# Where tiles lie in SBUF: weight slots and moving activation tiles put on fixed offsets modulo 256 bytes

## The chip, the cores and the metric

The kernel runs on one core of one Trainium2 chip. The metric is the device time of one execution in microseconds (us); several executions are timed and the median is given. Beside the times there is one execution taken by the hardware profiler, from which the tables below come. In them PE is the matrix engine (its matmuls), PEld its weight loads, DVE the vector engine, ACT the scalar engine, POOL the GpSimd engine and SP the engine that issues the DMAs. SBUF is the on-chip memory of 128 partitions; an address below is a byte within a partition, the same in all 128.

## The reference

The program is a two-layer encoder trunk on 256 tokens of width 1024, in float32. Each layer adds three sub-layers to the stream `h`: a gated feed-forward network (FFN) of width 2816, a token-mixing sub-layer with three head groups, and a second FFN. Before each stands an RMSNorm with a shift and scale computed from a vector `c`.

```python
for l in range(DEPTH):
    mod = (cond @ ada_w[l] + ada_b[l]).reshape(B, 9, D_MODEL)[:, None]
    u = modulate(rmsnorm(h, norm_ffn1[l]), mod[:, :, 0], mod[:, :, 1])
    h = h + 0.5 * (1.0 + mod[:, :, 2]) * swiglu(u, ffn1_wg[l], ffn1_wu[l], ffn1_wd[l])
    u = modulate(rmsnorm(h, norm_mix[l]), mod[:, :, 3], mod[:, :, 4])
    proj = u @ w_in[l]
    ...
    mixed = jnp.concatenate([y_ret, y_sb, y_ssm], axis=-1) @ w_out[l]
    h = h + (1.0 + mod[:, :, 5]) * mixed
    u = modulate(rmsnorm(h, norm_ffn2[l]), mod[:, :, 6], mod[:, :, 7])
    h = h + 0.5 * (1.0 + mod[:, :, 8]) * swiglu(u, ffn2_wg[l], ffn2_wu[l], ffn2_wd[l])
```

`swiglu(u, wg, wu, wd)` is `(silu(u @ wg) * (u @ wu)) @ wd`. Retention, stick-breaking attention and the state-space mixer, which lie between `proj` and `mixed`, are small beside the matrix products with the weights.

## The kernel before

**The matrix products.** Every product with a weight matrix is made from three matmuls in the format fp32r: weights and activations are each split into a high part (`hi`, `uh`, the first half of `g`) and a remainder (`lo`, `ul`, the second half of `g`), and `mm3` (L200) issues hi·high, hi·low and lo·high into one PSUM bank. The weight block of 128x128 is the stationary operand (512 bytes of a partition), the activation chunk of 128x256 is the moving one (1024 bytes). Each matmul has a weight load of its own, so that in an instruction stream of matmuls a weight load for the next one runs beside each of them.

**The stages.** An FFN goes through 11 units of 256 columns: `proj` (L548) computes gate `pg` and up `pu` for one unit from `uh` and `ul` (48 matmuls each), the gated result is split into a `g` tile (`gated`, L570), and `out_unit` (L498) multiplies a `g` tile of an earlier unit into `dn` (48 matmuls: 24 for the unit's first half, then 24 for its second). The first four chunks of work after each norm are done by `lead` (L452) on tiles `hgh` and `hgl`, that hold h before the norm factor is known, with two columns more (258). The mixing sub-layer projects 20 units (`pj`, or `pv` with the operands swapped: there the weights are the moving operand and `uh`, `ul` the stationary one) and ends with six units of `wo`, whose moving tiles are the pairs `rh`/`rl`, `bh`/`bl` and `sh`/`sl`.

**The weights.** A DMA on SP's queue brings one unit of 1 MB into a raw tile (four to ten of 8192 bytes per partition). `step` (L255) takes half a unit at a time: ACT writes `hi` (L306), DVE writes `lo` (L307). Pools `whi` and `wlo` have eight slots each, and half number k goes into slot k mod 8 of both. The stream of vectors for `mod` (`raw_a`, L266 on DVE) shares the raw tiles and the queue. The order of all instructions on all engines is written out by the program (`manual_schedule`).

**Where tiles lie.** A pool's slots follow each other in SBUF, and pools and constant tiles follow each other in the order in which they are declared; sizes are rounded up to 32 bytes. The first 16384 bytes are a scratch area for DMAs. A weight slot has 1056 float32, so 4224 bytes, which is 128 more than a multiple of 256: the eight slots of `whi` and of `wlo` lie in turn at 160 and 32 modulo 256 bytes. Chunks within a slot are 1024 bytes apart, weight blocks 512, so that they keep the slot's offset. `uh` and `ul` lie at 128. Pool `k4` has ten slots that are sized by the largest tile, 4x258 float32 or 4128 bytes; slot 0 begins at 160, and each further one 32 later: 160, 192, 224, 0, 32, 64, 96, 128, 160, 192. The tiles `g`, `rh` to `sl`, `hgh`, `hgl` and the activations of the mixing sub-layer take these slots in turn. In `hgh` and `hgl` chunks are 1032 bytes apart.

Of the kernel before, what the change touches and what calls it, by code (L numbers as in the profile page):

```python
# [7 lines left out]
F32 = mybir.dt.float32  # L8
FR = mybir.dt.float32r
# [4 lines left out]
P = 128  # L14
# [42 lines left out]

ONES, IDENT, LATER, HIDDEN = range(4)
GS = 3
MIX_UNITS = ['z0', 'z1', 'sk0', 'sv0', 'x0', 'sq0', 'x1', 'x2', 'sq1', 'sk1', 'rv0', 'sv1', 'x3', 'rq0', 'rg0', 'rv1', 'rg1', 'rk0', 'rk1', 'rq1']  # L60
PAUSE = {'step_sizes': (4, 2), 'conv': (3,), 'values': (6, 0), 'state_scores': (4, 2), 'ssm': (2, 2, 1, 2, 2, 2, 0, 4, 4, 2, 2), 'stick': (2, 2, 5, 3, 0, 3, 3, 1), 'rope': (2,), 'retain': (2, 2, 2, 0, 4, 3, 5, 2)}
W_OUT_ORDER = (2, 3, 5, 4, 0, 1)
# [3 lines left out]
def ffn_order(first=False):  # L66
    g0 = GS if first else 1
    seq = []
    for j in range(NJ):
        seq += [("g", j), ("u", j)]  # L70
        if j >= g0:
            seq += [("d", i) for i in downs(j, g0)]
    return seq + [("d", NJ - 1)]
# [10 lines left out]
def weight_order():  # L84
    seq = []
    for l in range(L):
        seq += [(l, "ffn1") + it for it in ffn_order(l == 0)]
        seq += [(l, "mix", "in", n) for n in MIX_UNITS]
        seq += [(l, "mix", "out", n) for n in W_OUT_ORDER]
# [12 lines left out]

HSEQ = [(_w, _f) for _f in range(2) for _w in range(2 * GS)]
PAIRS = LEADS[1:] + [_w + 2 for _w in LEADS[1:]]
for _w in range(2 * GS, NW):
    if _w in PAIRS:
# [10 lines left out]
def stream_order():  # L117
    after = {}

    def spread(first, last, count):  # L120
        for i in range(count):
            w = first + (i * (last - first)) // max(1, count)
            after[w] = after.get(w, 0) + 1

    base = 0
    for l in range(L):
        for off, span in zip((0, NF, NF + NM), ADA_SPANS[l]):
            spread(base + off + span[1], base + off + span[2], span[0])
        base += NSUB
    seq = []  # L130
    for it in START.split():
        if it[0] in "xsn":
            seq.append((it, 0, 0))
        elif it[0] == "a":
            seq.append(("a", int(it[1:]), 0))
        else:
            seq += [("w",) + h for h in HSEQ[2 * int(it):2 * int(it) + 2]]
    a = 8
    for n, hf in HSEQ[4 * GS:]:
        seq.append(("w", n, hf))  # L140
        if hf:
            for _ in range(after.get(n, 0)):
                seq.append(("a", a, 0))
                a += 1
    assert a == NA
    return seq


SEQ = stream_order()
START_SEQ = SEQ[:11 + 4 * GS]  # L150
UNIT_OF = {it: i // 2 for i, it in enumerate(HSEQ)}
# [4 lines left out]
class Trunk:  # L156
# [5 lines left out]
    def __init__(self, ctx, tc, io):  # L162
        self.tc, self.nc, self.io = tc, tc.nc, io
        pool = lambda name, bufs, **kw: ctx.enter_context(tc.tile_pool(name=name, bufs=bufs, **kw))
        self.cp = pool("const", 1)
        self.rawp = pool("raw", self.NRAW)
        self.hip = pool("whi", self.NHALF)
        self.lop = pool("wlo", self.NHALF)
        self.t2 = pool("t2", 5)
        self.sm = pool("small", 2)  # L170
        self.ring = pool("ringp", 4, space=PSUM)
        self.pool = pool
        self.early = tc.tile_pool(name="early", bufs=self.NEARLY)
        self.earlyp = self.early.__enter__()
        self.raw = {}
        self.w = {}
        self.sent = 0
        self.done = 0
        self.ready = -1
        self.procs = []  # L180
        self.table = None
# [36 lines left out]
    def acc2(self, name):  # L218
        return self.accp.tile([P, 2, 512], F32, tag="acc", name=name)

    def tk4(self, name, dt=F32, w=256):
        return self.k4.tile([P, 4, w], dt, tag="k4", name=name)

    def tk3(self, name, dt=F32):
        return self.t3.tile([P, 2, 384], dt, tag="t3", name=name)
# [29 lines left out]
    def step(self):  # L255
        nc = self.nc
        kind, n, hf = SEQ[self.done]
        self.done += 1
        unit = UNIT_OF[n, hf] if kind == "w" else n
        while (kind, unit) not in self.raw:  # L260
            self.send()
        raw = self.raw[kind, unit]
        if kind == "a":
            for f in range(2):
                j = 2 * n + f
                nc.vector.tensor_tensor_reduce(  # L266
                    out=raw[:, f * 1024:(f + 1) * 1024], in0=raw[:, f * 1024:(f + 1) * 1024], in1=self.cond,
                    scale=1.0, scalar=self.par("ada_b", j), op0=ALU.mult, op1=ALU.add,
                    accum_out=self.mods[:, j:j + 1])
            del self.raw[kind, n]  # L270
            self.send()
            return
        hi = self.hip.tile([P, 1056], FR, tag="hi", name=f"hi{n}_{hf}")
        lo = self.lop.tile([P, 1056], FR, tag="lo", name=f"lo{n}_{hf}")
        l, _, what, which = WSEQ[n]
        part = HPOS[n, hf] % 2
        src = raw[:, part * 1024:(part + 1) * 1024]
        if (what, which) == ("in", "sv0"):
            hv, lv = (t.rearrange("p (k c) -> p k c", c=264) for t in (hi, lo))
            self.split(hv[:, :, 0:256], lv[:, :, 0:256], src.rearrange("p (k c) -> p k c", c=256))  # L280
            self.split(hv[:, :, 256:264], lv[:, :, 256:264], self.wdt[:, l, 4 * hf:4 * hf + 4])
            self.w[n, hf] = (hv, lv)
        else:
            hv, lv = hi[:, 0:1024], lo[:, 0:1024]
            self.split(hv, lv, src)
            if what not in ("d", "out"):
                hv, lv = (t.rearrange("p (k c) -> p k c", c=256) for t in (hv, lv))
            self.w[n, hf] = (hv, lv)
        self.ready = HPOS[n, hf]
        if part:  # L290
            del self.raw[kind, unit]
            self.send()
# [16 lines left out]
    def setup(self):  # L309
        nc, io = self.nc, self.io  # L310
        self.params = self.cp.tile([P, NPAR], F32, name="params")
        self.consts = self.cp.tile([P, NCST], F32, name="consts")
        self.cond = self.cp.tile([P, 1024], F32, name="cond")
        self.wdt = self.cp.tile([P, L, 8, 8], F32, name="wdt")
        self.mods = self.cp.tile([P, NA * 2], F32, name="mods")
        self.h = self.cp.tile([P, KD, S], F32, name="h")
        self.uh = self.cp.tile([P, KD, S], FR, name="uh")
        self.ul = self.cp.tile([P, KD, S], FR, name="ul")
        self.rs = self.cp.tile([P, S], F32, name="rs")
        self.mats = self.cp.tile([P, 4, P], FR, name="mats")  # L320
        self.eps = self.cp.tile([P, 1], F32, name="eps")
        nc.vector.memset(self.eps, EPS)
        nc.sync.dma_start(out=self.cond, in_=io["c"].broadcast_to([P, 1024]))
        nc.sync.dma_start(out=self.params, in_=io["params"])
        for _ in range(self.NRAW + self.NEARLY + 1):
            self.send()
        self.silu(out=self.cond, in_=self.cond)
# [16 lines left out]
    def norm_prep(self, gain, gi, shift, scale, lead=True):  # L344
        nc = self.nc
        self.gs = self.sm.tile([P, 8], F32, tag="gs", name="gs")
        nc.vector.scalar_tensor_tensor(out=self.gs, in0=self.mods[:, scale:scale + 8], scalar=1.0,
                                       in1=self.par(gain, gi, 8), op0=ALU.add, op1=ALU.mult)
        self.shift = shift
        self.sq = []  # L350
        self.hg = None
        if lead:
            self.hg = [(self.tk4("hgh", FR, 258), self.tk4("hgl", FR, 258)) for _ in range(2)]
            for i, (hi, lo) in enumerate(self.hg):
                src = self.mods[:, shift + 4 * i:shift + 4 * i + 4].unsqueeze(2).to_broadcast([P, 4, 2])
                self.split(hi[:, :, 256:258], lo[:, :, 256:258], src)

    def start(self, gain, gi, shift, scale):
# [5 lines left out]
        nps = self.acc("nps")  # L364
        banks = [self.bank("ld") if i < 4 else self.acc("ld") for i in range(2 * GS)]
        units, steps, new = 2 * GS, [0] * 8, [0] * 4
# [260 lines left out]
    def mix(self, l, w0, gate_col, prep):  # L627
# [299 lines left out]
        n = w0 + 2  # L927
        for idx, name in enumerate(MIX_UNITS):
            if idx < 2:
                continue  # L930
            done = []
            if idx == 2:
                ts = [target(name), target(MIX_UNITS[3])]
                self.proj2(n, *ts)
                done = [evac(name, ts[0]), evac(MIX_UNITS[3], ts[1])]
            elif idx > 3:
# [158 lines left out]
```

## Time and profile before

| | |
|---|---|
| time, median of 3 runs | 1163.01 us (1162.42 to 1163.47) |
| profiled execution, first to last instruction (span) | 1161.9 us, 22045 instructions |
| mean granted TensorE clock | 0.998 |
| PE matmuls busy | 1126.8 us, 97% of the span, 9316 matmuls |
| DVE busy | 893.3 us, 77% |
| ACT busy | 619.0 us, 53% |
| HBM read | 280.15 MB, 242 GB/s over the span |

Matmuls are pipelined: one's duration in the profile (280 ns) overlaps with the next one's, so the rate of the stream is read from the distance between the starts of matmuls and not from durations. The timeline prints the start of each row, and a row "x2" is two matmuls of the same tiles in a row. For the unit of an FFN it is enough to look at the first matmul of 24 and the one that follows the 24th.

### The profile page before, as it was taken

Reading aid. Unit: us, or ns where it says so; the run is one execution under the profiler, and the core shown is the slowest. Engines: PE = TensorE matmul, PEld = TensorE weight load, DVE = VectorE, ACT = ScalarE, POOL = GpSimd, SP = SyncE. Lnnn points to the kernel's source line nnn. Section 1 sums busy time; section 2 is a strip of 40 time slices with the busy share of each in tenths; the row PEclk is TensorE's granted clock in tenths of the full one; section 3 lists DMA queues with packets and bytes.
Section 4 is the critical chain, followed back from the end, with each engine's and each line's share of the span. In section 5 each row is a group of like instructions: output and inputs, shape, how many; then the busy total and the mean of one; then the engine's idle time right before and its main releaser. Section 6 shows DMA issues by size and latency. Waiting matters only on the chain.

```text
span 1161.9 us, 22045 instructions
## 1 busy us (share of the span) xinstructions
PE 1126.8 (97%) x9316; PEld 1115.7 (96%) x9316; DVE 893.3 (77%) x1300; ACT 619.0 (53%) x870; POOL 0.2 (0%) x4
## 2 busy tenths in 40 slices
PE   1999999999999999999999999999999999999996
PEld 1999999999999999999999999999999999999996
DVE  6988786788778788898488788667886877977544
ACT  4464434586874464444466444457687546544432
POOL 0000000000000000000000000000000000000000
PEclk9999999999999999999999999999999999999999
DMA  9879898357454539999536988643655452987610
GB/s 376 338 265 366 320 361 333 129 214 276 163 190 155 182 142 370 347 372 359 188 110 258 345 322 307 254 182 144 256 182 186 177 189 80 351 331 283 235 58 37
DMA packets 39555, 282.63 MB, mean 243 GB/s; under 512 B 4384, under 2 KB 4640, under 8 KB 5408
## 3 DMA queue, kind: packets, MB, share of 16 engines
q1 hardware_dynamic: 39456, 281.22, 64.6%
q8 instruction: 73, 1.20, 0.4%
q14 instruction: 26, 0.21, 0.1%
HBM read 280.15 MB, written 1.05 MB: 242 GB/s over the span
## 4 chain that ended last, share of the span: by engine, by line
PE 96%; DVE 2%; ACT 1%; DMA 1%; issue 0%; SPq 0%; ACTq 0%; DVEq 0%
PE dn L198 21%; PE pu L198 19%; PE pg L198 19%; PE pj L198 14%; PE ld L198 7%; PE wo L198 6%; PE pv L198 4%; DVE raw_a L266 1%; PE seg L198 1%; PE nps L198 1%; DMA h<-in_x 1%; PE tail L198 1%; PE sz L198 1%; PE rn L198 1%; PE yb L198 1%; PE rs L198 0%
## 5 line engine op out<-in xcount | busy, mean ns | idle before, releaser
L307 DVE TENSOR_TENSOR lo<-raw_w,hi 128x1024 fp32r<-128x1024 f32 x368 | 441.6, 1222 | 152.8 <-ACT hi L306 152.5
L306 ACT ACTIVATE hi<-raw_w 128x1024 fp32r<-128x1024 f32 x368 | 380.3, 1053 | 252.4 <-DMA raw_w<-in_w 118.1
L198 PE MATMUL dn<-g,hi 128*128 128x256 f32 x1408 | 250.7, 280 | 0.0
L198 PEld LDWEIGHTS dn<-g,hi 128*128 128x128 f32 x1408 | 215.7, 189 | 0.0
L266 DVE CUSTOM_DVE_ANT_0 raw_a<-raw_a,cond,params 128x1024 f32<-128x1024 f32 x160 | 198.8, 1280 | 0.3 <-DMA raw_a<-in_ada 0.3
L198 PE MATMUL dn<-g,lo 128*128 128x256 f32 x704 | 197.3, 280 | 0.0
L198 PE MATMUL pu<-uh,hi 128*128 128x256 f32 x608 | 171.2, 282 | 0.0
L198 PE MATMUL pu<-ul,hi 128*128 128x256 f32 x608 | 171.2, 282 | 0.0
L198 PE MATMUL pg<-ul,hi 128*128 128x256 f32 x608 | 171.1, 281 | 0.0
L198 PE MATMUL pg<-uh,hi 128*128 128x256 f32 x608 | 171.1, 281 | 0.0
L198 PE MATMUL pg<-uh,lo 128*128 128x256 f32 x608 | 170.9, 281 | 0.0
L198 PE MATMUL pu<-uh,lo 128*128 128x256 f32 x608 | 170.8, 281 | 0.0
L198 PEld LDWEIGHTS dn<-g,lo 128*128 128x128 f32 x704 | 132.8, 189 | 0.0
L198 PE MATMUL pj<-uh,hi 128*128 128x256 f32 x448 | 127.9, 285 | 0.0
L198 PE MATMUL pj<-ul,hi 128*128 128x256 f32 x448 | 126.0, 281 | 0.0
L198 PE MATMUL pj<-uh,lo 128*128 128x256 f32 x448 | 125.9, 281 | 0.0
L198 PEld LDWEIGHTS pu<-uh,lo 128*128 128x128 f32 x608 | 114.9, 189 | 0.0
L198 PEld LDWEIGHTS pg<-uh,lo 128*128 128x128 f32 x608 | 114.8, 189 | 0.0
L198 PEld LDWEIGHTS pu<-ul,hi 128*128 128x128 f32 x608 | 114.5, 188 | 0.0
L198 PEld LDWEIGHTS pg<-ul,hi 128*128 128x128 f32 x608 | 114.4, 188 | 0.0
L198 PEld LDWEIGHTS pg<-uh,hi 128*128 128x128 f32 x608 | 114.4, 188 | 0.0
L198 PEld LDWEIGHTS pu<-uh,hi 128*128 128x128 f32 x608 | 114.3, 188 | 0.0
(189 smaller groups left out, 1791.2 us busy)
## 6 DMA issues: line engine op xcount, KB each, us to landing
raw_w<-in_w SPq DMA_DIRECT2D x184, 1024.0 KB, 5.8
raw_a<-in_ada SPq DMA_DIRECT2D x80, 1024.0 KB, 6.5
consts<-in_consts SPq DMA_DIRECT2D x1, 1216.0 KB, 10.1
h<-in_x SPq DMA_DIRECT2D x1, 1024.0 KB, 7.0
out<-fin SPq DMA_DIRECT2D x4, 256.0 KB, 2.3
cond<-in_c SPq DMA_DIRECT2D x1, 512.0 KB, 4.3
mats<-in_mats SPq DMA_DIRECT2D x1, 256.0 KB, 7.1
params<-in_params SPq DMA_DIRECT2D x1, 176.0 KB, 4.4
```

Of the source, the lines that this page charges most:

```text
L198: self.nc.tensor.matmul(out, lhsT=lhsT, rhs=rhs, start=start, stop=True, skip_group_check=True)
L266: nc.vector.tensor_tensor_reduce(out=raw[:, f * 1024:(f + 1) * 1024], in0=raw[:, f * 1024:(f + 1) * 1024], in1=self.cond, scale=1.0, scala ...
L306: self.nc.scalar.activation(out=hi, in_=src, func=AF.Copy)
L307: self.nc.vector.tensor_tensor(out=lo, in0=src, in1=hi.bitcast(F32), op=ALU.subtract)
```

## The change

The change alters sizes and paddings of tiles, and the size of the DMA scratch area. No instruction is added, taken away or moved: on each engine the same operations stand in the same order on tiles of the same names, at other addresses.

| tile | offset mod 256 before | after |
|---|---|---|
| eight slots each of `hi`, `lo` | 160 and 32 in turn | 32, all |
| `uh`, `ul` | 128 | 224 |
| ten slots of `k4` (`g`, `hgh`, `hgl`, `rh`..`sl` and others) | 160, 192, 224, 0, 32, 64, 96, 128, 160, 192 | 224, all |
| chunk distance in `hgh`, `hgl` | 1032 bytes | 1280 bytes |
| raw tiles | 160 | 32 (four) and 224 (early ones) |
| `t2` tiles (`sg`, `sq` and others) | 160 | 32 |
| `mats` | 128 | 32 |
| `t3` tiles | 224 | 224 |

```diff
+SCRATCH = 1024
+WSLOT = 1088
+KSLOT = 1280
+PAD_U = 24
+PAD_MATS = 16
+PAD_RAW = 56
+PAD_K4 = 48
...
         self.sm = pool("small", 2)
+        self.pad(pool("pads", 1), PAD_K4, "pad_k4")
...
-    def tk4(self, name, dt=F32, w=256):
-        return self.k4.tile([P, 4, w], dt, tag="k4", name=name)
+    def tk4(self, name, dt=F32):
+        t = self.k4.tile([P, KSLOT], dt, tag="k4", name=name)
+        return t[:, 0:1024].rearrange("p (a b) -> p a b", b=256)
+
+    def tk4x(self, name):
+        t = self.k4.tile([P, KSLOT], FR, tag="k4", name=name)
+        return t.rearrange("p (a b) -> p a b", b=320)[:, :, 0:258]
+
+    def pad(self, pool, n, name):
+        pool.tile([P, n], F32, name=name)
...
-        hi = self.hip.tile([P, 1056], FR, tag="hi", name=f"hi{n}_{hf}")
-        lo = self.lop.tile([P, 1056], FR, tag="lo", name=f"lo{n}_{hf}")
+        hi = self.hip.tile([P, WSLOT], FR, tag="hi", name=f"hi{n}_{hf}")
+        lo = self.lop.tile([P, WSLOT], FR, tag="lo", name=f"lo{n}_{hf}")
...
-            hv, lv = (t.rearrange("p (k c) -> p k c", c=264) for t in (hi, lo))
+            hv, lv = (t.rearrange("p (k c) -> p k c", c=264) for t in (hi[:, 0:1056], lo[:, 0:1056]))
...
+        self.pad(self.cp, PAD_U, "pad_u")
         self.uh = self.cp.tile([P, KD, S], FR, name="uh")
         self.ul = self.cp.tile([P, KD, S], FR, name="ul")
         self.rs = self.cp.tile([P, S], F32, name="rs")
+        self.pad(self.cp, PAD_MATS, "pad_mats")
         self.mats = self.cp.tile([P, 4, P], FR, name="mats")
         self.eps = self.cp.tile([P, 1], F32, name="eps")
+        self.pad(self.cp, PAD_RAW, "pad_raw")
...
-            self.hg = [(self.tk4("hgh", FR, 258), self.tk4("hgl", FR, 258)) for _ in range(2)]
+            self.hg = [(self.tk4x("hgh"), self.tk4x("hgl")) for _ in range(2)]
...
-    nc = bacc.Bacc("TRN2", target_bir_lowering=False, num_devices=1)
+    nc = bacc.Bacc("TRN2", target_bir_lowering=False, num_devices=1, dynamic_dma_scratch_size=SCRATCH)
```

## The prediction

> **What bounds the kernel now.** First the chain of work that ended last, by line, and the busy time by stage (in the stages: length, then PE, PEld, DVE, ACT and POOL busy with their instruction counts, the granted clock, the DMA engines' busy share, GB/s).
>
> ```profile
> by line: PE dn L198 21.3%; PE pu L198 18.7%; PE pg L198 18.7%; PE pj L198 13.9%; PE ld L198 7.5%; PE wo L198 5.9%; PE pv L198 3.9%; DVE raw_a L266 0.8%; PE seg L198 0.8%; PE nps L198 0.6%; DMA h<-in_x 0.6%; PE tail L198 0.6%; PE sz L198 0.6
> ...
> 93.00:210.00 117.00, 117.00 (x989) 117.00 (x988) 91.68 (x112) 50.09 (x55) 0.00 (x0) 1.00 0.89 333
> 423.00:545.00 122.00, 122.00 (x1030) 122.00 (x1029) 109.65 (x136) 55.28 (x63) 0.00 (x0) 1.00 0.92 352
> 620.00:780.00 160.00, 160.00 (x1350) 160.00 (x1349) 120.33 (x150) 73.47 (x88) 0.00 (x0) 1.00 0.79 296
> ```
>
> The seven first entries, all matmuls with weights, are 89.9% of the chain. In each of three FFN stages PE has no gap, at clock 1.00: 117.00 us for 989 matmuls, 122.00 for 1030, 160.00 for 1350, so 118.3 to 118.5 ns from one start to the next. Shortening that distance shortens the program, until DVE (busy 109.65 of 122.00 us) or the DMAs (0.92) bind. Number of matmuls behind each entry:
>
> ```profile
> L198 PE MATMUL dn<-g,hi 128*128 128x256 f32 x1408 | 250.7, 280 | 0.0
> L198 PE MATMUL dn<-g,lo 128*128 128x256 f32 x704 | 197.3, 280 | 0.0
> L198 PE MATMUL pg<-uh,hi 128*128 128x256 f32 x608 | 171.1, 281 | 0.0
> L198 PE MATMUL pj<-uh,hi 128*128 128x256 f32 x448 | 127.9, 285 | 0.0
> L198 PE MATMUL ld<-hgh,hi 128*128 128x258 f32 x160 | 46.6, 291 | 0.0
> L198 PE MATMUL ld<-uh,hi 128*128 128x256 f32 x96 | 28.3, 294 | 10.3 <-ACT hi L306 10.3
> L198 PE MATMUL pv<-hi,uh 128*128 128x256 f32 x96 | 27.2, 283 | 0.0
> L198 PE MATMUL wo<-rh,lo 128*128 128x256 f32 x64 | 17.9, 280 | 0.0
> ```
>
> `dn` has 2112; `pg`, `pu` 3x608 = 1824 each; `pj` 3x448 = 1344; `ld` 3x(160+96) = 768; `wo` nine such groups, 576; `pv` 384 (3x96, and the 3x32 of 264 columns). Shares of 1161.9 us, divided by these: `dn` 247.5 us, 117.2 ns each; `pg` and `pu` 434.6 us, **119.1 ns**; `pj` 161.5 us, 120.2; `wo` 68.6 us, 119.0; `pv` 45.3 us, 118.0.
>
> **Does the distance depend on the addresses?** The kernel before answers that by itself, since `dn` runs through ten `k4` slots. Below are halves of `dn` units: 24 matmuls of one kind from the first row to the second. Pairs are given as (moving, weights) modulo 256, from the rotation of the slots.
>
> ```profile
> 546.63 0.39 PE L198 MATMUL dn<-g,hi 128*128 128x256 f32 x2
> ...
> 549.35 0.28 PE L198 MATMUL pg<-uh,hi 128*128 128x256 f32 x1
> ```
>
> (224, 32), the only pair that is left after the change: 2.72 us, **113.3 ns**. Other pairs:
>
> ```profile
> 543.80 0.40 PE L198 MATMUL dn<-g,hi 128*128 128x256 f32 x2
> ...
> 546.63 0.39 PE L198 MATMUL dn<-g,hi 128*128 128x256 f32 x2
> ...
> 1106.65 0.40 PE L198 MATMUL dn<-g,hi 128*128 128x256 f32 x2
> ...
> 1109.53 0.28 PE L198 MATMUL pg<-uh,hi 128*128 128x256 f32 x1
> ...
> 560.78 0.40 PE L198 MATMUL dn<-g,hi 128*128 128x256 f32 x2
> ...
> 563.66 0.40 PE L198 MATMUL dn<-g,hi 128*128 128x256 f32 x2
> ...
> 566.50 0.28 PE L198 MATMUL pg<-uh,hi 128*128 128x256 f32 x1
> ```
>
> The same moving tile with weights at 160, (224, 160): 2.83 us, 117.9 ns. (32, 32): 2.88, 120.0. (128, 32): 2.88, 120.0. (128, 160): 2.84, 118.3. The same operation of the same shape, in one unit and its neighbour, takes 113.3 or 117.9 with nothing changed but the weights' slot. `pg` and `pu` read `uh`, `ul` at 128 with weights in turn at 32 and 160: the mean of 120.0 and 118.3 is 119.2, and their share gave 119.1. So what `dn` shows of a pair holds for other tiles too, and I carry 113.4 ns (the half with its borders) over to every stage.
>
> The Trainium skill says otherwise: in "TensorE: Matmul & The Clock Gate", section "Part 2: What happens when you issue a matmul", PE has separate SBUF read ports for the moving operand and for weights, and "Loading the next tile's weights doesn't steal SBUF read bandwidth from the running matmul." By that rule the slots would not matter and the time would stay at 1163. The rows above disagree with it: 113.3 against 117.9 ns.
>
> **The change part by part.**
> - `dn`: 2112 x (117.2 - 113.4) = 8.0 us. `pg`, `pu`: 3648 x 5.7 = 20.8. `pj`, at `pg`'s 119.1, since its share holds jumps to small matmuls: 1344 x 5.7 = 7.7. `wo`: 576 x 5.6 = 3.2. `ld`, at the same 5.7, its two further columns before and after alike: 768 x 5.7 = 4.4. Sum **44.1 us**.
> - `pv` becomes (32, 224) for most of its units, a pair that nothing shows with the operands in these roles. Bounds are 113.3 and 120.0, the ends of the rows above: 1.8 us won to 0.8 lost. Nearest is (224, 160), 64 apart as this one is, with 117.9; I take 116.5, between it and the fast row: 0.6 won.
> - Small float32 matmuls of attention and scan (`seg`, `tail`, `sz` and others) get other pairs too. `seg`, `tail` and `sz` together are 2.0% of the chain, 23 us; the spread of the rows (113.3 to 120.0) on that is at most 1.3 us either way. I take 0.
> - DVE and ACT write the weight slots. Two `lo` rows, slots at 160 and 32:
>
> ```profile
> 223.56 1.22 DVE L307 TENSOR_TENSOR lo<-raw_w,hi 128x1024 fp32r<-128x1024 f32 x1
> ...
> 228.34 1.22 DVE L307 TENSOR_TENSOR lo<-raw_w,hi 128x1024 fp32r<-128x1024 f32 x1
> ```
>
> Both 1.22 us: no effect. Raw tiles go from 160 to 32 or 224 mod 256, which no row compares. Bounds: 0, if the transfers keep their pace, and if some slowed, the cover is the stock of finished halves; I take 0.
> - The DMA scratch area: all DMAs here are issued by SP, so what it is for isn't used; 15360 bytes are 60 x 256, so this alone moves no tile modulo 256. Cost 0.
>
> **What is late next.** A faster PE needs its operands sooner. The tightest places follow a norm:
>
> ```profile
> 421.28 2.94 ACT L306 ACTIVATE hi<-raw_w 128x1024 fp32r<-128x1024 f32 x3
> 422.36 2.36 DVE L307 TENSOR_TENSOR lo<-raw_w,hi 128x1024 fp32r<-128x1024 f32 x2 [0.26 <-ACT hi L306]
> ...
> 424.28 0.28 PE L198 MATMUL dn<-g,lo 128*128 128x256 f32 x1
> ...
> 228.48 0.70 PE L198 MATMUL nps<-diag,mats 128*128 128x256 f32 x2 [0.16 <-DVE diag L341]
> ```
>
> The first `lo` of the row at 422.36 ends near 423.6 (1.22 long), its matmul starts at 424.28: 0.7 us to spare. PE runs some 120 matmuls between the norm's matmul and there, which now take 120 x 5.7 = 0.7 us less: just used up. PE already waits 0.16 us for the norm factor, behind 12 matmuls that become 0.07 us shorter. Five norms, 0.1 us each for both: **0.5 us lost**. Elsewhere splits wait for PE to give a slot free and are ahead:
>
> ```profile
> ACT hi L306 <- PE dn L198: 43.5, 28, 1.9
> ```
>
> In the stage from 423 to 545 us 1030 matmuls become 5.9 us faster: DVE's 109.65 us of 116.1 are 94%, the DMAs' 0.92 x 122 = 112 us are 97%. That fits, barely.
>
> Sum: -44.1 - 0.6 + 0.5 = -44.2 us. The profiled execution spans 1161.9 us, the median of the runs is 1.1 above it, 1163.0. 1161.9 - 44.2 + 1.1 = **1119 us**.
>
> **The rivals.**
> 1. *The fast rhythm does not hold everywhere.* The moving slot at 96 mod 256 shows both: (96, 160), as far apart as (224, 32) modulo 256, once took 2.75 us for 24 and once 2.82.
>
> ```profile
> 122.08 0.41 PE L198 MATMUL dn<-g,hi 128*128 128x256 f32 x2
> ...
> 124.83 0.39 PE L198 MATMUL dn<-g,hi 128*128 128x256 f32 x2
> ...
> 426.87 0.40 PE L198 MATMUL dn<-g,hi 128*128 128x256 f32 x2
> ...
> 429.69 0.28 PE L198 MATMUL pg<-uh,hi 128*128 128x256 f32 x1
> ```
>
> So one pair can run at 113 to 115 or at 117.5, by how it was entered. (224, 32) is seen only right after (224, 160). If half the stages settle at 117.8, half of 8448 x 4.4 ns = 37 us is missing: 1138; if all do, 1156.
> 2. *Another engine becomes the bound.* If DVE or the DMAs stop the stages 423 to 545 and 93 to 210 from gaining anything, (1030 + 989) x 5.7 = 11.5 us are missing: 1131. Against it: only 94% and 97% in the tighter one.
> 3. *Nothing changes.* The differences between halves of `dn` then come from something else that goes with the slot, for instance what ran just before, and 113.3 stays a rare case: 1163. Against it, that `pg` and `pu` agree with `dn`. (The rule of the Trainium skill quoted above would give this time.)
> 4. *Slower.* In (224, 32) the high and low moving halves lie 2048 bytes apart; `uh` and `ul` lie 8192 apart, and `hi` now also lies at 288 modulo 512 under a moving tile at 224, which no row has. If this locks into the rhythm of (32, 32), 120.0 for every matmul: `dn` 2112 x 2.8 = 5.9, `pg` and `pu` 3648 x 0.9 = 3.3, the other three 2688 x 0.9 = 2.4, so 11.6 us: 1175. It decides once the mean of the 8448, now 118.8, is over 119.1 (2.3 us more).
>
> **How the numbers follow.** About 0.2% (2.3 us) is what a measurement of this kernel can tell from no change. Forecast 65% (its own range 1113 to 1126: weight loads alone, in the row below, follow each other (0.86 - 0.19) / 6 = 112 ns apart, 1.4 less than assumed, so 8448 x 1.4 = 12 us would be the most beyond; half of it is taken). Rival 1: 15%. Rival 2: 8%. Rival 3: 7%. Rival 4: 5%. Faster 0.65 + 0.15 + 0.08 = 0.88, same 0.07, slower 0.05. The range for 8 in 10 goes from 1113 to 1146: all of the forecast, rival 2, and over half of rival 1.
>
> ```profile
> 225.84 0.86 PEld L198 LDWEIGHTS nps<-mats,sq 128*128 128x128 f32 x7
> ```
>
> **What would show it.** Right: 48 matmuls of `pg` in 5.44 us, with 5.72 before; halves of `dn` alike in all slots; three FFN stages with no PE gap. Wrong: halves of 2.83 us beside halves of 2.72 (rival 1); waits of PE on `hi` or `lo` (rival 2); `pg` at 5.72 (rival 3) or 5.76 (rival 4).

## The result and the profile after

| | before | after |
|---|---|---|
| time, median | 1162.98 us (1162.42 to 1163.47) | 1130.85 us (1124.4 to 1137.11) |
| ratio | | 0.9724, 95% interval 0.9687 to 0.976 |
| span of the profiled execution | 1161.9 us | 1129.0 us |
| mean granted TensorE clock | 0.998 | 0.998 |
| PE matmuls busy | 97% | 97% |

The change makes the kernel 2.8% faster. The time lies in the predicted range (1113 to 1146), but 12 us above the predicted 1119, and outside the 1113 to 1126 that the likeliest case alone allowed. Something else is new: the four executions took 1124.4, 1130.79, 1130.91 and 1137.11 us, in steps of about 6.3 us, where those of the kernel before lie within 1.1 us. Ratios leave out runs over 1.5% above the fastest of their kernel; that concerns two of the six of e6, below, alone.

The chain of work that ended last, of the changed kernel, by line:

```profile
by line: PE dn L206 21.3%; PE pg L206 18.5%; PE pu L206 18.5%; PE pj L206 13.8%; PE ld L206 7.6%; PE wo L206 6.0%; PE pv L206 3.9%; DVE raw_a L282 0.9%; PE seg L206 0.8%; PE nps L206 0.7%; PE tail L206 0.6%; PE sz L206 0.6%; DMA h<-in_x 0.6
```

The same seven entries lead, with almost the same shares: all of them shrank, by different amounts. Shares times 1129.0 us, against those of before (a share is rounded to 0.1%, some 0.6 us):

| entry | forecast gain, us | measured gain, us |
|---|---|---|
| `dn` | 8.0 | 247.5 - 240.5 = 7.0 |
| `pg` and `pu` | 20.8 | 434.6 - 417.7 = 16.9 |
| `pj` | 7.7 | 161.5 - 155.8 = 5.7 |
| `wo` | 3.2 | 68.6 - 67.7 = 0.9 |
| `ld` | 4.4 | 87.1 - 85.8 = 1.3 |
| `pv` | 0.6 | 45.3 - 44.0 = 1.3 |
| norms | -0.5 | not seen |
| sum | 44.2 | 33.1 (the span: 32.9) |

Where the rest is shows in one piece of each of the four FFN stages, in which PE does nothing but these matmuls (length, then PE, PEld, DVE, ACT and POOL busy with their instruction counts, clock, DMA share, GB/s). After:

```profile
100.00:200.00 100.00, 100.00 (x884) 100.00 (x884) 83.48 (x101) 43.88 (x49) 0.00 (x0) 1.00 0.94 357
420.00:560.00 140.00, 140.00 (x1238) 140.00 (x1237) 118.80 (x145) 64.10 (x73) 0.00 (x0) 1.00 0.92 349
605.00:750.00 145.00, 145.00 (x1234) 145.00 (x1232) 108.37 (x128) 63.87 (x73) 0.00 (x0) 1.00 0.79 300
965.00:1100.00 135.00, 135.00 (x1194) 135.00 (x1193) 98.45 (x110) 62.13 (x69) 0.00 (x0) 1.00 0.70 265
```

Length by count gives the distance between starts: 113.1 ns in the first, second and fourth stage, 117.5 in the third. (Two or three matmuls that still run at the left border are counted too, so these quotients come out about 0.2 ns low.) PE has no gap in any, and the clock is 1.00 in all. So three stages run as forecast and one does not. The same stretch of the kernel before has 1224 matmuls:

```profile
605.00:750.00 145.00, 145.00 (x1224) 145.00 (x1223) 113.51 (x138) 70.22 (x80) 0.00 (x0) 1.00 0.78 293
```

In e2, below, where this stage is in the shorter distance, it has 1282, 48 more than here; 48 matmuls by 113.3 ns are 5.4 us in 145 us, and 6.2 us over the stage from 593 to 757 us. That is one step of the spread above.

The distance stays the same for most of a stage. Here are the starts of 48 matmuls of `pg` in the first stage, and of the first 24 of `dn` in the third (timeline: start, length, engine, line, operation):

```profile
62.89 0.28 PE L206 MATMUL pg<-uh,hi 128*128 128x256 f32 x1
...
68.33 0.28 PE L206 MATMUL pu<-uh,hi 128*128 128x256 f32 x1
```

```profile
592.09 3.50 DVE L323 TENSOR_TENSOR lo<-raw_w,hi 128x1024 fp32r<-128x1024 f32 x3 [0.26 <-ACT hi L322]
...
593.13 0.28 PE L206 MATMUL pu<-uh,lo 128*128 128x256 f32 x1
593.24 0.39 PE L206 MATMUL dn<-g,hi 128*128 128x256 f32 x2
593.47 0.28 PE L206 MATMUL dn<-g,lo 128*128 128x256 f32 x1
...
596.06 0.40 PE L206 MATMUL dn<-g,hi 128*128 128x256 f32 x2
```

5.44 us for 48 is the forecast to the last digit, 113.3 ns. In the third stage the matmuls of `pu` just ahead still follow each other in 0.11 us; from the first `dn` on 24 take 2.82 us, 117.5 ns, and so it stays to the end of the stage. In every row of the changed kernel's stages the offsets are the same, (moving, weights) = (224, 32). One pair, two rhythms: 113.3 ns, called fast below, and 117.8 ns, called slow. At the place of the switch the first `lo` of the three is ready near 592.09 + 3.50 / 3 = 593.26 and the first matmul that uses it starts at 593.47: 0.2 us to spare, of the 0.7 before. In the second stage it is as late (a row of three from 410.11, 3.50 us long; first use at 411.49), and there three matmuls stand 122, 121 and 116 ns apart and the next ones 113 or 114 again. The same push has two outcomes.

The other gaps: the lead's 258 columns, and `wo`.

```profile
569.04 0.28 PE L206 MATMUL ld<-hgh,hi 128*128 128x258 f32 x1
...
574.84 0.28 PE L206 MATMUL ld<-hgh,hi 128*128 128x258 f32 x1
```

```profile
370.00:384.00 14.00, 14.00 (x122) 14.00 (x120) 9.17 (x14) 5.91 (x8) 0.00 (x0) 1.00 0.66 256
```

48 matmuls of the lead take 5.80 us, 120.8 ns, a little more than the 119.9 that the same groups had on the mean in the kernel before, by their starts in the trace. In 14 us of `wo` stand 122 matmuls; in e10, below, 126.

### The profile page after: what moved, and what is told of

Read it like the earlier page. It is cut to its first block, busy times and chain, and to the rows that moved or that the text cites. A ratio compares the mean times of both kernels' runs of the same rounds, so it can differ in the third digit from the quotient of the medians.

```text
span 1129.0 us, 22045 instructions
## 1 busy us (share of the span) xinstructions
PE 1094.3 (97%) x9316; PEld 1083.1 (96%) x9316; DVE 892.1 (79%) x1300; ACT 617.4 (55%) x870; POOL 0.2 (0%) x4
## 4 chain that ended last, share of the span: by engine, by line
PE 96%; DVE 2%; ACT 1%; DMA 1%; issue 0%; SPq 0%; ACTq 0%; DVEq 0%
PE dn L206 21%; PE pg L206 18%; PE pu L206 18%; PE pj L206 14%; PE ld L206 8%; PE wo L206 6%; PE pv L206 4%; DVE raw_a L282 1%; PE seg L206 1%; PE nps L206 1%; PE tail L206 1%; PE sz L206 1%; DMA h<-in_x 1%; PE rn L206 1%; PE yb L206 1%; PE rs L206 0%
## 5 line engine op out<-in xcount | busy, mean ns | idle before, releaser
L206 PE MATMUL dn<-g,hi 128*128 128x256 f32 x1408 | 243.6, 277 | 0.0
L206 PEld LDWEIGHTS dn<-g,hi 128*128 128x128 f32 x1408 | 212.9, 188 | 0.0
L282 DVE CUSTOM_DVE_ANT_0 raw_a<-raw_a,cond,params 128x1024 f32<-128x1024 f32 x160 | 198.9, 1280 | 0.0
L206 PE MATMUL pg<-ul,hi 128*128 128x256 f32 x608 | 168.6, 277 | 0.0
L206 PE MATMUL pg<-uh,hi 128*128 128x256 f32 x608 | 168.6, 277 | 0.0
L206 PE MATMUL pg<-uh,lo 128*128 128x256 f32 x608 | 168.5, 277 | 0.0
L206 PE MATMUL pu<-uh,hi 128*128 128x256 f32 x608 | 168.5, 277 | 0.0
L206 PE MATMUL pu<-ul,hi 128*128 128x256 f32 x608 | 168.5, 277 | 0.0
L206 PE MATMUL pu<-uh,lo 128*128 128x256 f32 x608 | 168.5, 277 | 0.0
```

Of the source, the lines that this page charges most:

```text
L206: self.nc.tensor.matmul(out, lhsT=lhsT, rhs=rhs, start=start, stop=True, skip_group_check=True)
L282: nc.vector.tensor_tensor_reduce(out=raw[:, f * 1024:(f + 1) * 1024], in0=raw[:, f * 1024:(f + 1) * 1024], in1=self.cond, scale=1.0, scala ...
```

## The experiments

The theory at the start (called A in what was expected): the distance is set by the offsets of the moving and the weight operand together; under 224 and 32 two rhythms are possible, and what pushes the stream from one to the other decides how long a stage takes. Rivals: only the weight slots matter, only the moving offset matters, or neither. Offsets are modulo 256 bytes, times in us.

| kernel | moving | `hi` | `lo` | median (range) |
|---|---|---|---|---|
| before | 128, `k4` all | 32, 160 in turn | as `hi` | 1162.98 (1162.42 to 1163.47) |
| changed | 224 | 32 | 32 | 1130.85 (1124.4 to 1137.11) |
| e1 | 128, `k4` all | 32 | 32 | 1168.79 (1168.18 to 1169.18) |
| e2 | 224 | 32, 160 in turn | as `hi` | 1124.82 (1124.4 to 1125.15) |
| e3 | 224 | 160 | 160 | 1151.85 (1150.49 to 1152.36) |
| e4 | 224 | 224 | 224 | 1173.64 (1173.33 to 1174.53) |
| e5 | 96 | 160 | 160 | 1136.98 (1136.81 to 1137.34) |
| e6 | as changed, earlier split | | | 1138.01 (1124.7 to 1145.44) |
| e7 | as e6, lead on 256 columns | | | 1133.11 (1129.56 to 1142.39) |
| e9 | as e2, earlier split | | | 1124.20 (1123.56 to 1124.99) |
| e10 | 224 | 32 | 160 | 1122.16 (1121.92 to 1122.57) |
| e11 | 224, `ul` 96 | 32 | 160 | 1160.88 (1160.29 to 1161.47) |
| e12 | 128 | 64 | 192 | 1144.64 (1139.87 to 1155.78) |
| e13 | 96 | 160 | 32 | 1122.52 (1121.78 to 1123.36) |

### e1: the weight slots alone

```diff
 the changed kernel, but:
-PAD_RAW = 56
+PAD_RAW = 80
-        self.pad(self.cp, PAD_U, "pad_u")
-        self.pad(pool("pads", 1), PAD_K4, "pad_k4")
 tk4 and the lead's tiles as in the kernel before (ten rotating slots, 258 columns)
```

> Only the weight slots of the change: every hi and lo slot at 32 mod 256, while uh and ul stay at 128 and the moving tiles of dn rotate through all offsets as in the kernel before. Theory A (the distance between matmuls is set by moving and weights offset together): pg, pu, pj, wo run the pair (128, 32) at 120.0 ns in place of 119.1, 5568 x 0.9 = 5 us lost; dn shows 113.3 in the slots at 224 alone and other distances in others, 3 us either way. Sum 1163 to 1171, no gain at all. Rival B (equal weight slots are what the gain comes from, whatever the moving tile): pg at 113.3 to 114.5 and 1125 to 1140 us. Rival C (the offsets are not the cause, the gain comes from the 1 KB scratch, which is in this kernel too): 1131 us.

Measured: 1168.79 us, ratio 1.0054 (1.0039 to 1.0069). The weight slots alone lose a little, as theory A has it; B and C fall. The 1 KB scratch area is in this kernel, so it does not carry the gain. In the second stage the profile of e1 has

```profile
420.00:560.00 140.00, 140.00 (x1175) 140.00 (x1174) 118.84 (x145) 64.90 (x75) 0.00 (x0) 1.00 0.88 331
```

119.1 ns. `dn` here runs through all moving offsets against one weight offset, 32. Of these eight only 96 and 224 ever show 113.3 ns, and each shows the slow distance in other units. These are two whole units of `dn`, 48 matmuls each, both in the `k4` slot at 224:

```profile
121.62 0.39 PE L205 MATMUL dn<-g,hi 128*128 128x256 f32 x2
...
127.06 0.28 PE L205 MATMUL pg<-uh,hi 128*128 128x256 f32 x1
...
424.77 0.40 PE L205 MATMUL dn<-g,hi 128*128 128x256 f32 x2
...
430.42 0.29 PE L205 MATMUL pg<-uh,hi 128*128 128x256 f32 x1
```

5.44 us (113.3 ns) and 5.65 us (117.7 ns), with the same tiles, addresses modulo 256 and order. So the offsets allow a rhythm, they don't impose it.

### e2: the moving tiles alone

```diff
-WSLOT = 1088
+WSLOT = 1056
```

> Only the moving tiles of the change: all at 224 mod 256, and weight slots of 4224 bytes that stand at 32 and 160 in turn. Theory A: halves alternate between 113.3 ns (224, 32) and 117.8 ns (224, 160), mean 115.6, so 8448 x (118.8 - 115.6) = 27 us are won, 1136 us, and up to 1142 if the lead's 258 columns gain nothing. Each half takes its own distance at once, 2.72 or 2.83 us for 24, so that no stage stays in the slow rhythm and repeated runs lie close together. Rival B (equal weight slots alone make the gain): no gain, 1163. Rival D (the moving offset alone makes it): 113.3 in every half, 1124 to 1131.

Measured: 1124.82 us, ratio 0.9675 (0.9659 to 0.9691): 6 us faster than the changed kernel, and runs within 0.8 us. No theory expected this with its reason. B falls; A's figure of 1136 falls too, since halves at 160 run at 113.3 ns as those at 32 do. D's time is met, but e3 and e4 below disprove D. What e2 has that the changed kernel lacks is a change of the weight offset at the border of each half:

```profile
411.39 0.39 PE L206 MATMUL dn<-g,hi 128*128 128x256 f32 x2
...
414.23 0.39 PE L206 MATMUL dn<-g,hi 128*128 128x256 f32 x2
...
416.95 0.28 PE L206 MATMUL pg<-uh,hi 128*128 128x256 f32 x1
...
605.00:750.00 145.00, 145.00 (x1282) 145.00 (x1281) 112.96 (x139) 66.58 (x78) 0.00 (x0) 1.00 0.83 309
```

The first half of this `dn` unit (weights at 160) was pushed into the slow rhythm, 2.84 us; the second (weights at 32) is fast again, 2.72 us. In the last FFN stage of e2 the stream is slow for 96 matmuls, and again comes back where weights at 32 follow weights at 160 (at the second such border). With one weight offset for all, the changed kernel was in the slow rhythm for 1392 matmuls. This gave a new theory, A2: both weight offsets allow both rhythms, and a change of the weight offset is a way out of the slow one. It is not a sure one. In this last stage the stream stayed slow at the first border from 160 to 32 (955.49 us) and at the one from 32 to 160 (961.15 us). In the kernel before, the half of rival 1 in the prediction that is slow at (96, 160) from 426.87 us follows a half at (96, 32) that was slow too.

### e3 and e4: other offsets for all weights

```diff
 e3
-PAD_RAW = 56
-PAD_K4 = 48
+PAD_RAW = 88
+PAD_K4 = 16
 e4
-PAD_RAW = 56
-PAD_K4 = 48
+PAD_RAW = 104
+PAD_K4 = 64
```

> The changed kernel with all weight slots at 160 mod 256 in place of 32; the moving tiles stay at 224 and all slots stay equal modulo 256. Theory A: the pair (224, 160) gives 117.8 ns in every stage: 8448 x (118.8 - 117.8) = 8 us won, 1153 to 1157 us. Rival D (the moving offset alone): as the changed kernel, 1124 to 1137. If 160 has two rhythms as well, halves of 2.72 us stand beside halves of 2.83 and the time lies between.

> The changed kernel with all weight slots at 224 mod 256, where the moving tiles are too. Theory A: equal offsets run as (32, 32) did in the kernel before, 120.0 ns: 8448 x 1.2 = 10 us lost, 1170 to 1176 us, slower than before. Rival D (the moving offset alone) and rival E (any layout in which all slots of a kind are alike is fast): 1124 to 1137.

Measured: e3 1151.85 us, ratio 0.9907 (0.9892 to 0.9922); e4 1173.64, ratio 1.0098 (1.0083 to 1.0113). e4 is in theory A's range and e3 1 us below its range of 1153 to 1157; D and E fall. With every moving tile at 224 the time goes from 1122 (e10, below) to 1174 us by the weights' offsets alone. One line of e3, one of e4:

```profile
605.00:750.00 145.00, 145.00 (x1233) 145.00 (x1233) 113.51 (x132) 69.08 (x77) 0.00 (x0) 1.00 0.81 301
...
605.00:750.00 145.00, 145.00 (x1211) 145.00 (x1210) 115.23 (x147) 70.24 (x84) 0.00 (x0) 1.00 0.79 294
```

117.6 and 119.7 ns. In the profiled run of e3 all four FFN stages are at 117.8, and by the times in the other runs too, though e2 shows halves of the same pair (224, 160) at 113.3: this, too, is a slow rhythm that nothing ended, so A's time was nearly met and its reason, that this pair has 117.8 always, was not. Four slow stages of about 6.5 us above 1124.4, the shortest run of the changed kernel, give 1150.4. In e4 no stage is faster than 120 ns.

### e6: an earlier split, against the push

```diff
         self.apply_b(KD - 1, us[KD - 1])
+        self.need(n + 1, 1, 5)
         for f in range(4):
             ends(f, ts[f], bias[:, f:f + 1])
```

> The changed kernel with one line more: in the lead, the first half of the first dn unit is split into hi and lo before the products of sg, not after them, so that its lo is written some 1.2 us earlier. Theory A (the stream is pushed out of the fast rhythm by the wait of the first dn matmuls for this lo): no FFN stage begins slow, the stage from 593 us on runs at 113.3 ns and wins 1392 x 4.45 ns = 6.2 us; 1122 to 1126 us in every run, runs within 2 us of each other. Rival F (the rhythm falls out at random, whatever lo does): runs still differ in steps of about 6 us, 1124, 1131 or 1137.

Measured: six runs, 1124.7, 1130.9, 1137.56, 1138.47, 1144.3 and 1145.44 us; ratio 0.9742 (0.9706 to 0.9778). This is a miss for theory A in the form that it had. The push at the first `dn` is gone, but the steps are not, and the profiled run has two slow stages in place of one:

```profile
401.09 0.28 PE L206 MATMUL pg<-uh,hi 128*128 128x256 f32 x1
...
402.50 0.28 PE L206 MATMUL pg<-uh,hi 128*128 128x256 f32 x1
...
420.00:560.00 140.00, 140.00 (x1191) 140.00 (x1191) 116.24 (x141) 60.78 (x69) 0.00 (x0) 1.00 0.90 343
605.00:750.00 145.00, 145.00 (x1282) 145.00 (x1281) 114.12 (x133) 69.36 (x76) 0.00 (x0) 1.00 0.84 314
965.00:1100.00 135.00, 135.00 (x1149) 135.00 (x1148) 97.11 (x109) 62.13 (x69) 0.00 (x0) 1.00 0.71 265
```

The third stage (605 to 750) is now fast, as expected. But the second and the fourth are slow from their very first `pg` on: 12 matmuls in 1.41 us, 117.5 ns. So a late `lo` is one way into the slow rhythm. The passage from the lead's 258 columns to the first `pg` is another: the first one to seven matmuls there are off the fast distance even where the stage then runs fast. Which rhythm they settle on, nothing in the trace foretells. Rival F is right about the entry, not about what comes after it: with one moving offset of 224 or 96 and one weight offset, no FFN stage was seen to leave the slow rhythm once it had held it for half a unit.

### e9: the earlier split with two weight offsets in turn

> Weight slots of 4224 bytes (32 and 160 in turn, as in the run with the moving tiles alone) together with the earlier split. Theory A: the pushes at the first dn units go, of which that run still had two (24 and 96 slow matmuls, 0.5 us); wo and pj keep their mixture. 1122.5 to 1125 us. If equal slots were worth something beside the moving offset, this would be slower than the changed kernel with the earlier split by more than 2 us; by theory A the two lie within 2 us.

It is e6 with `WSLOT = 1056`. Measured: 1124.20 us, ratio 0.9668 (0.9655 to 0.968), in the range that A gave. No FFN stage has a slow piece behind its first few matmuls. Against e2 it is 0.6 us faster, the size of the two pushes (24 and 96 matmuls by 4.45 ns, 0.5 us), which is not more than the runs of either differ. A also expected e9 and e6 within 2 us of each other, and that is a miss: e9 is 14 us below e6 in the median, by the width of the weight slots alone. Equal slots are worse, not better.

### e7: the lead on 256 columns

```diff
-            self.mm3(banks[f][:, 0:258], ..., (gh[:, k % 4], gl[:, k % 4]), k == 0)
+            self.mm3(banks[f][:, 0:256], ..., (gh[:, k % 4, 0:256], gl[:, k % 4, 0:256]), k == 0)
...
-            nc.scalar.activation(out=bias[:, f:f + 1], in_=banks[f][:, 256:257], func=AF.Copy)
+            nc.scalar.activation(out=bias[:, f:f + 1], in_=banks[f][:, 0:1], func=AF.Copy, scale=0.0)
```

> The earlier split, and the lead's matmuls on 256 columns in place of 258; the two columns that carry the shift part are left out, and the bias made from them is zero. Theory A with its explanation of the lead (258 moving columns do not fit the fast rhythm): the 480 lead matmuls go from 120.8 to 113.4 ns, 3.5 us less than the run with the earlier split alone, 1118 to 1122 us. Rival G (the lead is at 120 because it goes back and forth between two weight units and two high and low tiles, six matmuls at a time): only the two columns are saved, 2 / 258 of 120.8 ns is 0.9 ns each, 0.5 us less.

Measured: 1133.11 us (1129.56 to 1142.39), so the time misses what A expected, since this kernel too has stages that fell into the slow rhythm; the total cannot decide here. The lead itself can:

```profile
568.40 0.28 PE L206 MATMUL ld<-hgh,hi 128*128 128x256 f32 x1
...
573.84 0.28 PE L206 MATMUL ld<-hgh,hi 128*128 128x256 f32 x1
...
386.77 0.28 PE L206 MATMUL ld<-hgh,hi 128*128 128x256 f32 x1
...
392.42 0.28 PE L206 MATMUL ld<-hgh,hi 128*128 128x256 f32 x1
```

In the first pair of rows 5.44 us for the 48 matmuls that took 5.80 in the changed kernel: 113.3 ns in place of 120.8. The two columns are 0.9 ns of the 7.5 by their share, the rest is the rhythm. But only two of the five leads do so; the other three, as in the second pair, take 5.65 us, 117.8 ns; the stream was slow already when it came to them. Even these are 3.0 ns faster than 258 columns, so G falls. 256 columns make the fast rhythm possible in the lead, they don't ensure it. The groups of 258 columns were in no profiled run below 118.6 ns over 48 matmuls; why is open. The third FFN stage of e7 is slow from its first `pg` on (1234 matmuls from 605 to 750 us), with no 258 columns ahead of it: these are not the only cause of that way in.

### e10: `hi` at 32, `lo` at 160

```diff
+        self.pad(pool("padlo", 1), 32, "pad_lo")
         self.lop = pool("wlo", self.NHALF)
...
-PAD_K4 = 48
+PAD_K4 = 16
```

> The changed kernel with all lo slots at 160 mod 256 and all hi slots at 32, so that the weight offset changes within every three matmuls. Theory A2 (both offsets allow the fast rhythm under 224, and each change of the offset gives a stream that has fallen out a chance to come back): FFN stages at 113.3 ns throughout and also wo and pj nearer to it than in the changed kernel; 1118 to 1125 us. Rival H (a change of the weight offset costs time itself): over 115 ns on the mean of a stage, 1135 us or more. Rival I (the pairs are what counts, (224, 32) fast and (224, 160) slow): one of three matmuls at 117.8, mean 114.8, 1135 to 1139 us.

Measured: 1122.16 us, ratio 0.965 (0.9637 to 0.9662), runs within 0.7 us. A2 is met in the time, the spread and the stages; H and I fall. Two stretches of e10, the push at the first `dn` of its third FFN stage, and its return to the fast rhythm in `wo` after a small matmul:

```profile
370.00:384.00 14.00, 14.00 (x126) 14.00 (x125) 9.85 (x17) 7.07 (x11) 0.00 (x0) 1.00 0.67 248
605.00:750.00 145.00, 145.00 (x1282) 145.00 (x1281) 112.90 (x143) 66.74 (x80) 0.00 (x0) 1.00 0.82 309
```

```profile
591.58 0.39 PE L207 MATMUL dn<-g,hi 128*128 128x256 f32 x2
...
592.29 0.39 PE L207 MATMUL dn<-g,hi 128*128 128x256 f32 x2
...
594.34 0.39 PE L207 MATMUL dn<-g,hi 128*128 128x256 f32 x2
```

```profile
346.12 0.82 PE L207 MATMUL ry<-rp,rv 128*128 128x256 f32 x4
346.70 0.36 PE L207 MATMUL wo<-bh,hi 128*128 128x256 f32 x1
346.90 0.28 PE L207 MATMUL wo<-bl,hi 128*128 128x256 f32 x1
...
347.86 0.28 PE L207 MATMUL wo<-bh,hi 128*128 128x256 f32 x1
...
348.76 0.28 PE L207 MATMUL wo<-bh,lo 128*128 128x256 f32 x1
```

The first six matmuls of that `dn` take 0.71 us (118 ns), the next 18 take 2.05 (114): the push that cost the changed kernel a stage is over at once. In `wo`, from 346.90, eight matmuls take 0.96 us (120 ns), and from 347.86 eight take 0.90 (113): out of the disturbance within ten matmuls. In the changed kernel `wo` stays slow for its last 234 matmuls, past two more small ones. Start to start in the trace, without the jumps over 130 ns, `wo` falls from 117.3 to 113.8 ns and `pj` from 114.9 to 114.0; `pv`, whose moving operand now has two offsets, rises from 115.3 to 118.7.

### e12, e5: other offsets with the same differences

```diff
 e12, from e10
-        self.pad(self.cp, PAD_U, "pad_u")
-PAD_MATS = 16
-PAD_RAW = 56
-PAD_K4 = 16
+PAD_MATS = 40
+PAD_RAW = 64
+PAD_K4 = 48
 e5, from the changed kernel
-PAD_U = 24
+PAD_U = 56
```

> Every moving tile at 128 mod 256, as uh and ul are in the kernel before; hi slots at 64 and lo slots at 192, so that moving minus weights is 64 or 192 modulo 256, as in the run with lo at 160. Theory J (only the difference of the two offsets matters, and 64 or 192 allows the fast rhythm): the same as the run with lo at 160, FFN stages at 113.3 ns and 1121 to 1124 us. Rival K (224 is the offset that matters, or the 96 bytes of it that reach to the next 256): the moving offset 128 gave 118.3 to 120.0 ns in the kernel before with weights at 160 and 32, so 1155 to 1174 us.

> The changed kernel with all moving tiles and all weight slots shifted by 128 bytes, moving at 96 and weights at 160 mod 256, all slots alike as in the changed kernel. Theory J (the difference alone): two rhythms and no way out of the slow one, as the changed kernel: 1122 to 1145 us, FFN stages wholly at 113.3 or wholly at 117.8 ns, runs differing by steps of 6 to 7 us. Rival K (absolute offset): one fixed distance, at least 115 in all stages, and runs within 2 us of each other.

Measured: e12 1144.64 us, ratio 0.986 (0.9801 to 0.9918), runs from 1139.87 to 1155.78; e5 1136.98, ratio 0.978 (0.9766 to 0.9795), all four runs within 0.6 us. First and third stage of e12, then third and fourth of e5:

```profile
100.00:200.00 100.00, 100.00 (x884) 100.00 (x884) 84.26 (x104) 45.57 (x52) 0.00 (x0) 1.00 0.93 357
605.00:750.00 145.00, 145.00 (x1222) 145.00 (x1221) 107.31 (x127) 62.44 (x70) 0.00 (x0) 1.00 0.80 299
...
605.00:750.00 145.00, 145.00 (x1234) 145.00 (x1233) 108.02 (x128) 63.50 (x72) 0.00 (x0) 1.00 0.79 298
965.00:1100.00 135.00, 135.00 (x1149) 135.00 (x1148) 97.22 (x109) 61.09 (x68) 0.00 (x0) 1.00 0.72 265
```

e12 reaches 113.1 ns with moving tiles at 128, an offset at which the kernel before never did: rival K falls. But its slow rhythm is another one, 118.9 ns by the starts, and two of its stages, pushed at their first `dn`, don't come out of it for 1392 matmuls each, although `hi` and `lo` are 128 bytes apart as in e10. Its runs lie near 1140, 1148 and 1156 us, in steps close to the 7.8 us that 1392 matmuls by the 5.6 ns between its two rhythms make. So J falls as well: in these runs the difference of the offsets says whether the fast rhythm is possible, not what the slow one costs and how it ends. e5 has whole stages at 113.1 and at 117.5 ns, as J expected, but no steps between its runs: which stages are slow was here the same each time, or at least as many.

### e11: `ul` at 96

```diff
 e10, and:
+        self.pad(self.cp, 32, "pad_ul")
         self.ul = self.cp.tile([P, KD, S], FR, name="ul")
...
-PAD_MATS = 16
+PAD_MATS = 48
```

> The run with lo at 160, and ul moved to 96 mod 256 as well, so that moving minus weights is 192, 64, 64 in the three matmuls of uh and ul, where it was 192, 192, 64. g, the lead's tiles and rh, rl stay at 224. Theory J: every difference is still 64 or 192, so pg and pu stay at 113.3 ns; what pj and pv do after the small matmuls may shift by 1 to 2 us either way. 1120 to 1125 us. If the pattern of differences within the three decides which rhythm can hold, pg and pu leave 113.3: at 117.8, 3648 x 4.45 ns = 16 us more.

Measured: 1160.88 us, ratio 0.9984 (0.9975 to 0.9994), 39 us above e10 for one tile moved by 128 bytes. Within one kernel, `pg` and then `dn`, 48 matmuls of each:

```profile
86.76 0.28 PE L207 MATMUL pg<-uh,hi 128*128 128x256 f32 x1
...
92.55 0.28 PE L207 MATMUL pu<-uh,hi 128*128 128x256 f32 x1
...
101.10 0.39 PE L207 MATMUL dn<-g,hi 128*128 128x256 f32 x2
...
106.54 0.39 PE L207 MATMUL dn<-g,hi 128*128 128x256 f32 x2
```

5.79 us (120.6 ns) for `pg`, whose moving tiles are at 224 and 96 in turn; 5.44 us (113.3 ns) for `dn`, whose moving tile stays at 224. Every single pair is one that runs fast elsewhere; the sequence is not. J's 1120 to 1125 us are missed; the last sentence of the expectation holds, with 120.6 where it said 117.8.

### e13: e5 with `lo` moved

```diff
 e5, and:
+        self.pad(pool("padlo", 1), 32, "pad_lo")
         self.lop = pool("wlo", self.NHALF)
...
-PAD_K4 = 48
+PAD_K4 = 16
```

> The run with everything shifted by 128 bytes (moving at 96, all weights at 160; it held two FFN stages in the slow rhythm), with lo slots alone moved to 32 mod 256. Theory A2 (two weight offsets 128 bytes apart within every three matmuls, under one moving offset, end the slow rhythm wherever it begins): all FFN stages at 113.3 ns but for some tens of matmuls, wo near 114, 1121 to 1125 us, some 14 us less than with equal slots. Rival L (the run with lo at 160 was only lucky in where its streams restart): two FFN stages stay at 117.8 or 118.6 and the time stays within 1130 to 1145 us.

Measured: 1122.52 us, ratio 0.965 (0.9633 to 0.9666), 14.5 us below e5. A2 is met and L falls.

```profile
605.00:750.00 145.00, 145.00 (x1282) 145.00 (x1281) 113.16 (x141) 66.04 (x79) 0.00 (x0) 1.00 0.83 308
965.00:1100.00 135.00, 135.00 (x1194) 135.00 (x1193) 91.97 (x104) 61.25 (x68) 0.00 (x0) 1.00 0.66 244
```

Both stages that e5 held slow (1234 and 1149 matmuls) are fast. e10 and e13 are the fastest kernels of the study, some 9 us below the changed one, and their runs agree within 1.6 us.

## Why the prediction was right, and where it was not

- **The time.** It is in the range because the range took in over half of rival 1, not because the forecast came true: of the four runs one, 1124.4 us, lies in the forecast's own 1113 to 1126. Where in the range the median fell was in part chance, since it depends on how many stages went slow in each run.
- **The bound.** Right: PE without a gap at clock 1.00 before and after, and all the time that was won was won in the distance between matmuls.
- **The distance depends on the addresses.** Right, and now shown by e1 to e4: 1122 to 1174 us with nothing changed but addresses. The rule quoted from the Trainium skill, "TensorE: Matmul & The Clock Gate", Part 2, that loading the next weights takes no read bandwidth from the running matmul, would leave all of these at one time; e4 and e10 are 51 us apart, so these runs don't agree with it.
- **The step that failed** is the one that says "what `dn` shows of a pair holds for other tiles too, and I carry 113.4 ns (the half with its borders) over to every stage". A pair allows a rhythm and does not fix it. The rows of (224, 32) that carried it came from slots that follow (224, 160); the prediction noted that under rival 1 and gave it 15%. By e2 this was the point: the change of the weight offset from one slot to the next can bring a stream back, and the change under study removes it. Rival 1 is what happened, in one FFN stage of the profiled run (6.2 us by the count of its slow matmuls; the rounded shares of `dn`, `pg` and `pu` are 4.9 short), in most of `wo` (2.3 us less than forecast) and in part of `pj` (2.0 us less).
- **Mis-sized: the lead.** Forecast 4.4 us, measured 1.3. The groups of 258 columns, 480 of the 768, were at 120.8 ns, where they had been at 119.9; "the same 5.7" does not hold for them. e7 shows that 256 columns can take 113.3 or 117.8 there. `pv`, forecast 0.6, gave 1.3: 48 of its matmuls at the pair (32, 224), from 276.64 us, take 5.44 us, the fast distance, where 116.5 ns was assumed.
- **What is late next.** The place was right: at the first `dn` unit after a norm 0.2 us of the 0.7 are left. The price was not the 0.1 us that was assumed for a norm, but in one stage a push that put 1392 matmuls into the slow rhythm, and in another next to nothing. e6 shows that this push is one way in among others. The 0.5 us for norms was not seen.
- **Rival 2** fell: in the tighter stage, from 423 to 538 us, DVE is busy 103.68 of 115.00 us and the DMAs 0.96 with PE full, where 94% and 97% were forecast. **Rival 3** fell, and **rival 4** too as to this change; but its rhythm exists, and e4 shows its time: 1173.64, where 1175 was worked out for it.
- **Scratch.** Nothing to see, as assumed: e1 and e4 have it and are slower than the kernel before. It was not run alone.

What stays open: why a stream settles on one rhythm at a restart, why e12 and e11 behave unlike e10, and what in the memory or in PE makes the rhythms. The runs show when they come and go, not the mechanism. That e3's four slow stages and e5's two repeat in every run was read from the times alone, beside one profile each.

## What to carry to other kernels

In a kernel bound by back-to-back float32 matmuls with a weight load for each, write down the offsets modulo 256 bytes of moving and weight tiles, and read the distance between starts stage by stage: 113, 118 and 120 ns look alike in busy time (PE is 97% in all of them). Making all slots alike is not the aim: with one moving offset, 224 or 96, and high and low weights at 32 and 160, 128 bytes apart, the kernel was both the fastest and the steadiest (e10, e13), and equal slots left a stream in whatever rhythm it fell into. The 128 bytes are no rule by themselves: with moving tiles at 128 and weights at 64 and 192 (e12) stages stayed slow and the runs spread over 16 us. So measure the layout that is chosen. A time that comes in steps from run to run is a hint to look for a stage with two states.

## What was not expected of the hardware

- A stream keeps to one of a few distances. Three matmuls take 340 ns (fast), 353.3 (slow) or 360 (e4), so 113.3, 117.8 and 120.0 each; other offsets add 118.9 (e12) and 120.6 (e11).
- A stream of matmuls keeps its rhythm for over a thousand matmuls with one weight offset (1392 of them at 117.8 ns in the changed kernel) and the same pair of offsets shows both rhythms in one execution (e1: 5.44 and 5.65 us for 48).
- The fast rhythm was seen with moving minus weights at 64 or 192 modulo 256, and not at 0 (e4) or 96 (e1's `pg`); with two moving offsets in turn it was not seen even at 64 and 192 (e11).
- Two columns more, 258 for 256, cost 3.0 or 7.5 ns in the lead: 120.8 in the changed kernel, 117.8 or 113.3 in e7.
